# A streaming-encoder layer on one core: the last state-space unit is squeezed into twelve attention steps, the last fetch of its output moves from GpSimd's queue to SP's, and twenty low-part subtractions are queued behind a root

## The chip, the cores and the metric

The kernel runs on one core of one Trainium2 chip. The metric is the device time of one execution in microseconds. The time before is the median of three runs, 2292.37 us (2288.35 to 2292.53). The engines are called as in the profile: PE (TensorE), PEld (its weight loads), DVE (VectorE), ACT (ScalarE), POOL (GpSimd) and SP (SyncE, which issues most DMAs).

## What is computed

One layer over 2048 tokens of width 1024, in float32. Cut to what matters:

```python
h = rmsnorm(x, norm_mix_g);  proj = h @ w_in            # columns: u_ssm 512 | q 512 | k 512 | v 512
y_ssm = s5_mixer(u_ssm, ...)                            # 32 groups of 16 channels, one complex 64-state scan each
    # y = Re(C state) + D u;  y = gelu(y);  y = y * sigmoid(y @ w_glu + b_glu)
y_att = chunked_attention(q, k, v, rel_bias)            # 64-frame chunks, 8 chunks to the left, 8 heads
mixed = concat(rmsnorm(y_ssm, g1), rmsnorm(y_att, g2))
x  = x + mixed @ w_out
h2 = rmsnorm(x, norm_ffn_g)
x  = x + (silu(h2 @ w_gate) * (h2 @ w_up)) @ w_down
return rmsnorm(x, norm_final_g)
```

## The kernel before

**Precision and tiles.** Most products are made from float32 values split in two: a high part, cast by ACT (line 177, the helper `split`), and a low part, the raw value less the high one (line 178, on DVE or POOL). Each product is then three matmuls (line 77 is the helper through which PE's matmuls go, in program order; line 80 is the one for transposes). Tokens are worked on in four blocks `sb` of 512.

**Order.** All instructions of an engine run in one queue, in the order in which the program was laid out. PE's order, and that of the instructions issued through `k.V`, `k.A` and `k.Q`, is that of the code; the rest of DVE, ACT, POOL and SP is ordered by the scheduler of the framework, which has its own estimate of when an operand is ready. An instruction that waits holds back all that stands behind it on its engine.

**Attention with fillers.** `att_phase` runs 128 attention steps (block, pair of heads, head, 128 queries). A step's scores (`sc`) go from PE to DVE, which adds the bias `nb` and takes the minimum `mn` (line 858), then to ACT for the exponential (line 861). Two steps later PE transposes the result (`pt`), ACT copies its high part (`pth`, line 876), DVE its low part (`ptl`, line 877); after four steps `pv_head` multiplies by the values (`pj <- pth, ptl, v`; ACT `yt` line 900, DVE `ya` line 901). There is one buffer for `sc` and one for `pt`. Other work is put between the steps by `Unit.advance`: each unit is a generator with a first and a last step, and is carried on in proportion. Among the units are eight state-space units (`ssm_unit`, four groups each), one after the other, 15 steps each from step 2. One unit loads its tiles, makes `X` on PE and ACT, runs the scan on POOL (lines 617 to 629), sends the carried states to `XG` by four DMAs on POOL's queue (line 651), and after `YX` empty yields makes its output from eight matmuls, in turn `U, Tm` and `XG, Vm`. ACT copies that (line 661) and SP writes it to DRAM as `y` with eight DMAs (line 664).

**The mix phase.** At step `OPEN` = 119 `mix_phase` begins: SP loads the four row tiles of the GLU weights (`sg`, line 1006; two buffers), which ACT and DVE split into `wgh` and `wgl`. `load` fetches `y` in four tiles `f` of 128 channels (`yr`, line 1046), each by one DMA: for the first two blocks tiles 0 to 2 are on SP's queue and tile 3, which holds the channels of the last two units, is on POOL's. For the first two blocks the GELU is made of ACT square (line 1051), DVE (1052), ACT tanh (1053), DVE (1054), and its halves `gh` (ACT, line 1065) and `gl` (DVE, line 1066) are the operands of the GLU's matmuls (`pf <- gh, wgh` and so on), which PE runs between the last attention steps, tile 0 first.

**The third block's root and the gate.** After the output projection of a block (`w_out`, 2 x 24 matmuls for each of four column pairs `n`; DVE adds the residual in line 1140, SP stores it in line 1141, ACT squares it in lines 1143 to 1146, POOL adds up) `rstd_steps` makes the norm of that block: PE sums the squares (`big <- ones, sa`), `newton` makes the inverse root in ten small DVE instructions (lines 119 to 128, the last gives `no`), and PE spreads it by four transposes (`big <- ident, no`). For the third block (`sb` = 2) this lies inside the last block's output projection: the sum after `n` = 1 and the spread after `n` = 2. Behind `n` = 1 stands `build` as well, which fetches five of the seven first-half operands of the gate's product from DRAM (`lo <- hc`, line 1361, 5 x 4 DMAs) and splits them: twenty ACT casts (`hi`), twenty DVE subtractions (`lo`). The gate's first product then needs `hi`, `lo` and the split weights `c`; its first weight tile is cast by ACT and subtracted by DVE (line 178, `c <- raw`).

Of the kernel before, what the change touches and what calls it, by code (L numbers as in the profile page):

```python
# [16 lines left out]
P = 128  # L17
# [29 lines left out]
SL = 1  # L47
# [3 lines left out]
SW = 15  # L51
# [58 lines left out]
def f32(ap):  # L110
    return ap.bitcast(F32)
# [27 lines left out]
def spread(k, te, pb, o, c):  # L139

    for i in range(4):
        te.transpose(pb[:, i * P : (i + 1) * P], o[:, c + i : c + i + 1].to_broadcast([P, P]), k.ident[:])
# [525 lines left out]
SSM_N = YL + GP + 7 + 7 + 3 + 4  + YX + GP  # L668
# [24 lines left out]
def att_phase(k, ident, S):  # L693
    tc, nc, io = k.tc, k.nc, k.io
    with ExitStack() as cx:
# [245 lines left out]
        sp = tc.alloc_tile_pool(name="ssm", reuse_waits="tile", bufs=1)  # L941
        psum = cx.enter_context(tc.tile_pool(name="aps", bufs=1, space=bass.MemoryType.PSUM, reuse_waits="tile"))
        psum2 = cx.enter_context(tc.tile_pool(name="aps2", bufs=1, space=bass.MemoryType.PSUM, reuse_waits="tile"))
        units = []
# [9 lines left out]
                      Unit(qk_unit(sb, 2), QK_N, g0 + C[3], g0 + C[4], 2, light=LIGHT), Unit(v_unit(sb, 1), V_N, g0 + C[4], g0 + C[5], 2, light=LIGHT),  # L954
                      Unit(qk_unit(sb, 3), QK_N, g0 + C[5], g0 + C[6], 2, light=LIGHT)]
        for b in range(NG // GB):
            units.append(Unit(ssm_unit(k, sp, psum, S, b, k.ssm_eng), SSM_N, 2 + int(SW * b), 2 + int(SW * (b + 1)), light=SL))
        N = len(steps)
        for s in range(N + LAG + 2):
            if s == OPEN:  # L960
# [24 lines left out]
def mix_phase(k, S, bank):  # L985

    tc, nc, io = k.tc, k.nc, k.io
    te = k.te
    with ExitStack() as cx:
# [46 lines left out]
        yrs = [None]  # L1036

        def load(sb, early=False):
            b = B()
            b.o, b.early = {}, early  # L1040
            yt = k.t(my, "ys", [P, 4, SB], bufs=2)
            b.ys, b.g = [yt[:, f] for f in range(4)], []
            if sb % 2 == 0:
                yrs[0] = k.t(my, "yr", [P, 4, L, 128])
                for f in range(4):
                    (nc.gpsimd if sb == 0 and f == 3 else nc.sync).dma_start(yrs[0][:, f], S["y"][f * P : (f + 1) * P, :, sb * 64 : sb * 64 + 128])
            yv = yrs[0][:, :, :, (sb % 2) * 64 : (sb % 2 + 1) * 64]
            for f in range(4):
                if early:
                    t = k.t(mz, "tg", [P, L, SB // L], bufs=TGB)  # L1050
                    nc.scalar.activation(t[:], yv[:, f], AF.Square)
                    nc.vector.scalar_tensor_tensor(t[:], t[:], 1 / CUBE, yv[:, f], op0=ALU.add, op1=ALU.mult)
                    nc.scalar.activation(t[:], t[:], AF.Tanh, scale=CUBE * math.sqrt(2 / math.pi))
                    nc.vector.scalar_tensor_tensor(b.ys[f].rearrange("p (c j) -> p j c", j=L), t[:], 1.0, yv[:, f], op0=ALU.add, op1=ALU.mult)
                else:
                    nc.scalar.activation(yt[:, f].rearrange("p (c j) -> p c j", j=L), yv[:, f].rearrange("p j c -> p c j"), AF.Gelu_apprx_tanh)
            if sb != 1:
                halves(b)
            return b

        def halves(b):
            for f in range(4):
                gh, gl = k.t(my, f"gh{f}", [P, SB], F32R), k.t(my, f"gl{f}", [P, SB], F32R)
                if b.early:
                    nc.scalar.activation(gh[:], b.ys[f], AF.Copy, scale=0.5)
                    nc.vector.scalar_tensor_tensor(gl[:], b.ys[f], 0.5, f32(gh[:]), op0=ALU.mult, op1=ALU.subtract)
                else:
                    split(k, gh[:], gl[:], b.ys[f], nc.vector)
                b.g.append((gh, gl))
# [32 lines left out]
        def rstd2(b, c, pb):  # L1102

            for f, (y, g) in enumerate(zip((b.ya, b.ys)[c], (ga, gq if b.early else gs)[c : c + 1] * 4)):
                nc.vector.scalar_tensor_tensor(y, y, g[:, f : f + 1], pb, op0=ALU.mult, op1=ALU.mult)

        def big():
            return k.t(psum, *BIG)
# [10 lines left out]
        def mixed(b, c):  # L1119
            for n, (q, y) in enumerate(zip(QS[4 * c : 4 * c + 4], (b.ya, b.ys)[c])):  # L1120
                mt = k.t(mx, f"m{q}", [P, 2, SB], F32R)
                mh, ml = b.m[q] = mt[:, 0], mt[:, 1]
                split(k, mh, ml, y, nc.vector)
# [47 lines left out]
        b = load(0, True)  # L1171
# [26 lines left out]
        psum, mx = k.psum, k.mx  # L1198
# [6 lines left out]
        for sb in range(NSB):  # L1205
            if sb:
                b.m = {}
                mixed(b, 0)
            if sb == 0:
                held = [w_out(0, b, 2 * n) for n in range(2)]  # L1210
                next(held[0])
                ps = big()
                spread(k, te, ps[:, :512], b.o[1], 0)
                with tc.high_priority():
                    rstd2(b, 1, ps[:, :512])
                    mixed(b, 1)
                next(held[1])
            else:
                mixed(b, 1)
            for n in range(4):  # L1220
                if n == 0 and 0 < sb < NSB - 1:
                    nxt = next_block(sb + 1)
                if sb or n > 1:
                    for _ in w_out(sb, b, 2 * n):
                        pass
                else:
                    next(held[n])
                if n - (sb == NSB - 1) in (0, 1) and xr:
                    next(xr)
                if n in (1, 2) and sb + 1 < NSB:  # L1230
                    norm(nxt, n - 1)
                for _ in range(PRE0.get((sb, n), 0)):
                    next(pre)
                if (sb, n) == (NSB - 1, 1):
                    rx.close()
                    k.ga1 = tc.alloc_tile_pool(name="ga1", reuse_waits="tile", bufs=1, side="right")
                    k.gr = tc.alloc_tile_pool(name="gr", reuse_waits="tile", bufs=2, side="right")
                    wr = cx.enter_context(tc.tile_pool(name="wr2", reuse_waits="tile", bufs=2, side="right"))
                    k.hT = build(k, S, 0, k.ga1, EARLY)
            if sb < NSB - 1:  # L1240
                xr = rstd_steps(k, te, psum, k.mf, BIG, b.sa[:], D, S["rsn"][:, sb * SB : (sb + 1) * SB])
            if sb == 1:
                pre = pre_steps(k, S, 0, pre_tiles().__next__, True)
            k.last = b.sa[:]
            b = nxt
# [4 lines left out]
EARLY, LATE = (B11, T1, T2, B21, T3), (B22, T4)  # L1250
# [103 lines left out]
def build(k, S, hf, pool, ns):  # L1354

    hT = {}
    for n in ns:
        hi, lo = hT[n] = tuple(k.t(pool, f"{m}{n}", [P, 4, 512], F32R) for m in ("hi", "lo"))
        with k.tc.high_priority():
            for q in range(4) if hf == 0 else (slice(0, 4),):  # L1360
                k.nc.sync.dma_start(f32(lo[:, q]), S["hc"][hf, n, :, q])
        for q in range(4):
            split(k, hi[:, q], lo[:, q], f32(lo[:, q]), k.nc.vector)
    return hT
# [372 lines left out]
```

## Time and profile before

| What | Value |
|---|---|
| median of three runs | 2292.37 us (2288.35 to 2292.53) |
| the profiled execution: its time, its span | 2296.12 us, 2294.3 us |
| mean granted TensorE clock | 0.976 |
| busy: PE, PEld, DVE, ACT, POOL | 2180.3, 1835.1, 1490.5, 997.6, 1008.5 us |
| the chain that ended last: PE, DVE, issue, DMA | 76%, 8%, 6%, 5% |

The time is 1.8 us more than the span, which runs from the first to the last instruction. Times of single instructions below are microseconds from the span's start. In rows of the timeline, a bracket at the end holds the time for which the engine was idle before the row and what ended it; in rows of the waits stand the total, the number of times and the longest.

### The profile page before, as it was taken

The page shows a single profiled execution, that of the slowest core. Times are in us where ns is not written, and L with a number is a line of the kernel's source. Part 1 is how long each engine was busy: PE and PEld are TensorE (multiplying, and loading weights), DVE is VectorE, ACT ScalarE, POOL GpSimd, SP SyncE. Part 2 cuts the span into 40 slices and gives each one's busy share as a digit, 9 for nine tenths or more (in the row PEclk, how much of TensorE's full clock was granted, in tenths as well). Part 3 has the DMA queues.
Part 4 walks back from the last instruction along what each step waited for, and adds up shares of the span by engine and source line. Part 5 has one row for each costly group of instructions (what it writes and reads, how often), then busy time and mean ns, then how long its engine had stood idle before and what let it go on. Part 6 is the DMA issues. An engine that isn't in the chain of part 4 may idle for free.

```text
span 2294.3 us, 30408 instructions
## 1 busy us (share of the span) xinstructions
PE 2180.3 (95%) x10576; PEld 1835.1 (80%) x10576; DVE 1490.5 (65%) x2253; ACT 997.6 (43%) x1686; POOL 1008.5 (44%) x1215
## 2 busy tenths in 40 slices
PE   8978899899997999999999999999999999999998
PEld 6767688898986788778888887788888878888887
DVE  7845555656557755766775669766745376579576
ACT  6335455555556652343333335333333343345332
POOL 3406645356651121245555554555555414335450
PEclk9989999999998999999999999999999999999999
DMA  8887776676655334743554647454433297565552
GB/s 294 268 284 263 225 209 192 185 216 193 189 142 176 131 117 152 271 154 131 171 187 153 231 167 283 165 197 161 175 101 108 73 332 266 177 220 193 179 215 74
DMA packets 214769, 436.99 MB, mean 190 GB/s; under 512 B 27352, under 2 KB 57096, under 8 KB 207512
## 3 DMA queue, kind: packets, MB, share of 16 engines
q1 hardware_dynamic: 208728, 417.48, 54.8%
q0 software_dynamic: 5888, 17.58, 2.4%
q8 instruction: 83, 1.36, 0.3%
q14 instruction: 70, 0.57, 0.1%
HBM read 294.98 MB, written 132.15 MB: 186 GB/s over the span
## 4 chain that ended last, share of the span: by engine, by line
PE 76%; DVE 8%; issue 6%; DMA 5%; POOL 3%; ACT 2%; SPq 1%; DVEq 0%; POOLq 0%; ACTq 0%
PE X L77 19%; PE ps L77 18%; PE Y L77 10%; PE pf L77 8%; PE big L77 7%; PE W L77 5%; PE pj L77 4%; PE sc L77 2%; PE pt L80 2%; DMA xt<-in_xt 1%; DVE lo L178 1%; DMA lo<-hc 1%; DVE acc L1607 1%; SPq L579 1%; DMA w<-in_x 0%
## 5 line engine op out<-in xcount | busy, mean ns | idle before, releaser
L77 PE MATMUL X<-hi,c 128*128 128x512 f32 x1408 | 451.7, 391 | 5.0 <-ACT u L1415 2.9
L77 PE MATMUL ps<-hd,hd 128*128 128x512 f32 (+1 forms) x1968 | 428.2, 379 | 2.0 <-DVE hd L178 2.0
L77 PEld LDWEIGHTS ps<-hd,hd 128*128 128x128 f32 x1968 | 356.4, 188 | 72.4 <-DVE hd L178 3.1
L178 POOL TENSOR_TENSOR c<-S,c 128x512 fp32r<-128x512 f32 x172 | 246.4, 1435 | 268.9 <-ACT c L177 263.1
L77 PEld LDWEIGHTS X<-hi,c 128*128 128x128 f32 x1408 | 265.4, 189 | 62.6 <-ACT u L1415 4.9
L77 PE MATMUL X<-lo,c 128*128 128x512 f32 x704 | 274.9, 391 | 0.0
L178 POOL TENSOR_TENSOR hd<-hd 128x1536 fp32r<-128x1536 f32 (+1 forms) x46 | 157.0, 3416 | 215.3 <-ACT hd L177 204.4
L177 ACT CAST hd<-hd 128x1536 fp32r<-128x1536 f32 (+1 forms) x106 | 147.1, 1393 | 215.4 <-DMA hd<-hq 147.7
L178 POOL TENSOR_TENSOR c<-raw,c 128x512 fp32r<-128x512 f32 x129 | 185.8, 1441 | 123.5 <-ACT c L177 98.3
L77 PE MATMUL Y<-hi,c 128*128 128x512 f32 x704 | 225.7, 390 | 8.1 <-DVE u L1419 8.1
L1546 DVE TENSOR_TENSOR acc<-acc,ps 128x512 f32<-128x512 f32 x196 | 129.6, 682 | 77.8 <-PE ps L77 77.5
L77 PE MATMUL big<-m,woh 128*128 128x512 f32 x512 | 162.5, 399 | 1.4 <-DVE m L178 1.4
L77 PEld LDWEIGHTS Y<-hi,c 128*128 128x128 f32 x704 | 132.5, 188 | 37.7 <-DVE u L1419 10.2
L77 PE MATMUL pf<-hi,w 128*128 128x512 f32 x416 | 152.8, 420 | 7.4 <-ACT hi L741 3.9
L177 ACT CAST c<-S 128x512 fp32r<-128x512 f32 x176 | 109.4, 621 | 113.7 <-PE Y L77 51.3
L77 PEld LDWEIGHTS X<-lo,c 128*128 128x128 f32 x704 | 132.9, 189 | 27.4
L858 DVE CUSTOM_DVE_ANT_0 s<-sc,nb 128x640 f32<-128x640 f32 (+4 forms) x128 | 94.6, 739 | 91.5 <-PE sc L77 86.7
L617 POOL TENSOR_TENSOR st<-X,a 128x128 f32<-128x128 f32 (+2 forms) x136 | 46.0, 338 | 239.8 <-ACT X L603 204.7
L1415 ACT COPY u<-X 128x512 f32<-128x512 f32 x132 | 77.2, 584 | 159.8 <-PE X L77 159.8
L177 ACT CAST c<-raw 128x512 fp32r<-128x512 f32 x132 | 82.1, 622 | 139.9 <-PE Y L77 71.0
L178 DVE TENSOR_TENSOR hd<-hd 128x1536 fp32r<-128x1536 f32 (+1 forms) x60 | 118.1, 1969 | 30.6 <-ACT hd L177 30.2
L77 PE MATMUL Y<-lo,c 128*128 128x512 f32 x352 | 137.2, 390 | 0.0
(468 smaller groups left out, 4618.6 us busy)
## 6 DMA issues: line engine op xcount, KB each, us to landing
w<-wss SPq DMA_DIRECT2D x36, 1024.0 KB, 5.5
hq<-g SPq DMA_DIRECT2D x133, 256.0 KB, 2.1
hd<-hq SPq DMA_DIRECT2D x42, 768.0 KB, 4.5
hd<-wc SPq DMA_DIRECT2D x42, 768.0 KB, 6.0
raw<-in_w_gate SPq DMA_DIRECT2D x44, 512.0 KB, 3.8
raw<-in_w_up SPq DMA_DIRECT2D x44, 512.0 KB, 4.1
wc<-px SPq DMA_DIRECT2D x66, 256.0 KB, 3.2
wss<-w SPq DMA_DIRECT2D x12, 1024.0 KB, 5.6
```

The lines of the kernel that those rows point to most:

```text
L77: return self.tc.keep_in_program_order(self.tc.nc.tensor.matmul(*a, **b))
L80: return self.tc.keep_in_program_order(self.tc.nc.tensor.transpose(*a, **b))
L177: (hi_eng or nc.scalar).copy(hi, raw)
L178: (lo_eng or nc.gpsimd).tensor_tensor(lo, raw, f32(hi), op=ALU.subtract)
L579: ins = nc.sync.dma_start(out, in_)
L617: eng.tensor_tensor(t[:, :, :, :n], src, ar, op=ALU.mult)
L858: nc.vector.tensor_tensor_reduce(s[:, :nk].rearrange("p (a b) -> p a b", a=nch), ps[:, :nch, :half], hd.nb[:, nk - 1 :: -1].rearrange("p ( ...
L1415: nc.scalar.copy(u[:], ps[:])
L1546: V.tensor_tensor(a, a, ps[:], op=ALU.add)
L1607: nc.vector.scalar_tensor_tensor(v, v, k.go[:, i : i + 1], rs, op0=ALU.mult, op1=ALU.mult)
```

## The change

Three edits. First, the last step of a state-space unit is capped at 119; only the last unit (steps 107 to 122) is shortened by it, to twelve steps. Second, all four tiles of `y` go through SP's queue. Third, `build` for the first half runs inside `tc.issue_after(k.root)`, which puts every instruction of the block that runs on the root's engine, DVE, behind the root: `k.root` is at that place the last instruction of the third block's `newton`. The block's DMAs and ACT casts are not on DVE and are not held.

```diff
-            units.append(Unit(ssm_unit(k, sp, psum, S, b, k.ssm_eng), SSM_N, 2 + int(SW * b), 2 + int(SW * (b + 1)), light=SL))
+            units.append(Unit(ssm_unit(k, sp, psum, S, b, k.ssm_eng), SSM_N, 2 + int(SW * b), min(2 + int(SW * (b + 1)), 119), light=SL))
...
-                    (nc.gpsimd if sb == 0 and f == 3 else nc.sync).dma_start(yrs[0][:, f], S["y"][f * P : (f + 1) * P, :, sb * 64 : sb * 64 + 128])
+                    nc.sync.dma_start(yrs[0][:, f], S["y"][f * P : (f + 1) * P, :, sb * 64 : sb * 64 + 128])
...
-                    k.hT = build(k, S, 0, k.ga1, EARLY)
+                    with tc.issue_after(k.root):
+                        k.hT = build(k, S, 0, k.ga1, EARLY)
```

What it moves is seen in the order of the queues. On PE only the last unit's eight output matmuls move. In the kernel before, this stands on PE before them (the end of the last unit of key projections is above the first row; `sc` are scores, `pt` transposes):

```order
L77 MATMUL sc_8173<-k_1720_7352,q2l_7351 128x320
L80 MATMUL pt_8182<-ident_81,s_8077 128x128 x5
L77 MATMUL sc_8230<-k_1845_7976,q2h_7974 128x320
L77 MATMUL sc_8230<-k_1845_7976,q2l_7975 128x320
...
L80 MATMUL pt_8240<-ident_81,s_8124 128x128 x5
...
L80 MATMUL pt_8257<-ident_81,s_8178 128x128 x5
L77 MATMUL pj_8266<-U_7536,Tm_7547 128x256
L77 MATMUL pj_8266<-XG_2371,Vm_7556 128x256
...
L77 MATMUL sc_8289<-k_1845_7976,q2h_7974 128x320
```

In the changed kernel the same place on PE reads (`pf <- hi, w` are the last key projections):

```order
L77 MATMUL pf_8084<-lo_1554_6550,w_7883 128x512
L77 MATMUL pf_8084<-hi_1553_6549,w_7883 128x512
L77 MATMUL pj_8173<-U_7536,Tm_7547 128x256
L77 MATMUL pj_8173<-XG_2371,Vm_7556 128x256
...
L77 MATMUL pj_8179<-U_7536,Tm_7547 128x256
L77 MATMUL pj_8179<-XG_2371,Vm_7556 128x256
L77 MATMUL sc_8194<-k_1720_7352,q2h_7350 128x320
...
L80 MATMUL pt_8203<-ident_81,s_8093 128x128 x5
L77 MATMUL sc_8251<-k_1857_8012,q2h_8010 128x320
```

The eight matmuls have moved up past three score groups and three groups of transposes (27 instructions), directly behind the last key projection. On POOL nothing of the unit moves: its scan and its four `XG` DMAs stand where they did, and only the fetch of `y` is gone from its queue.

ACT's and DVE's orders change from there to the first GLU output. On ACT the kernel before has, around the transposes of the last head but one (`tg` the GELU, `gh` GLU operands; tiles 0 to 2 done, tile 3 at the end):

```order
L1065 ACTIVATE gh_1937_8368<-ys_8338 128x512
L1065 ACTIVATE gh_1939_8372<-ys_8338 128x512
L876 CAST pth_8322<-pt_8440 128x5x128
L861 ACTIVATE s_8429,sm_8237<-s_8429,mn_8430 128x640
L876 CAST pth_8322<-pt_8457 128x5x128
L861 ACTIVATE s_8453,sm_8237<-s_8453,mn_8454 128x640
L876 CAST pth_8322<-pt_8481 128x5x128
L861 ACTIVATE s_8477,sm_8237<-s_8477,mn_8478 128x640
L1026 ACTIVATE sq_8409<-ya_1948_8401 128x512
L1029 ACTIVATE sg_8411<-ya_1949_8402 128x512
L1051 ACTIVATE tg_8359<-yr_8339 128x512
```

The changed kernel has on ACT, at the same transposes:

```order
L876 CAST pth_8322<-pt_8440 128x5x128
L177 CAST wgh_1903_8239<-sg_8241 128x512
L876 CAST pth_8322<-pt_8457 128x5x128
L177 CAST wgh_1906_8245<-sg_8247 128x512
L1051 ACTIVATE tg_8349<-yr_8339 128x512
L861 ACTIVATE s_8453,sm_8258<-s_8453,mn_8454 128x640
L1053 ACTIVATE tg_8349<-tg_8349 128x512
L1051 ACTIVATE tg_8354<-yr_8339 128x512
L1065 ACTIVATE gh_1937_8368<-ys_8338 128x512
L1051 ACTIVATE tg_8359<-yr_8339 128x512
L1053 ACTIVATE tg_8354<-tg_8354 128x512
```

The GELU of tiles 1 and 2 has moved behind the transposes `pt_8457`, together with that of tile 3 and of the next block, and the exponentials and copies of the steps 8477 and 8481 stand behind all of these; DVE's order follows the same pattern. On SP the eight writes of `y` now stand ahead of the last two GLU weight loads, of the bias load `nb` for the next head and of the fetches of tiles 1 to 3.

On DVE, at the third block's root, the kernel before has the low parts in between (`lo_2249` and so on are the five operands, four subtractions each; line 1140 is the output projection's eviction):

```order
L1140 TENSOR_TENSOR xt_10152<-xt_10152,big_10154 128x1024
L178 TENSOR_TENSOR lo_2249_10339<-lo_2249_10339,hi_2248_10338 128x512
...
L178 TENSOR_TENSOR lo_2257_10395<-lo_2257_10395,hi_2256_10394 128x512
L178 TENSOR_TENSOR lo_2255_10381<-lo_2255_10381,hi_2254_10380 128x512
L119 TENSOR_SCALAR nv_10307<-big_10302 128x4
L1140 TENSOR_TENSOR xt_10246<-xt_10246,big_10248 128x1024
L120 TENSOR_SCALAR ny_10309<-nv_10307 128x4
...
L128 SCALAR_TENSOR_TENSOR no_10310<-nf_10308,ny_10309 128x4
...
L1140 TENSOR_TENSOR xt_10408<-xt_10408,big_10410 128x1024
L178 TENSOR_TENSOR lo_2249_10339<-lo_2249_10339,hi_2248_10338 128x512
L1140 TENSOR_TENSOR xt_10470<-xt_10470,big_10472 128x1024
```

The changed kernel has on DVE:

```order
L1140 TENSOR_TENSOR xt_10152<-xt_10152,big_10154 128x1024
L1140 TENSOR_TENSOR xt_10246<-xt_10246,big_10248 128x1024
L119 TENSOR_SCALAR nv_10307<-big_10302 128x4
...
L128 SCALAR_TENSOR_TENSOR no_10310<-nf_10308,ny_10309 128x4
L178 TENSOR_TENSOR lo_2249_10339<-lo_2249_10339,hi_2248_10338 128x512 x2
...
L178 TENSOR_TENSOR lo_2249_10339<-lo_2249_10339,hi_2248_10338 128x512
L178 TENSOR_TENSOR lo_2255_10381<-lo_2255_10381,hi_2254_10380 128x512
L178 TENSOR_TENSOR lo_2257_10395<-lo_2257_10395,hi_2256_10394 128x512 x4
L1140 TENSOR_TENSOR xt_10408<-xt_10408,big_10410 128x1024
L1140 TENSOR_TENSOR xt_10470<-xt_10470,big_10472 128x1024
```

The root and the eviction of `xt_10246` now stand ahead of all twenty low parts, and the eviction of `xt_10408` behind all twenty; before, 19 of them were ahead of it. The last cast on ACT is that of `lo_2249`; five subtractions now stand behind the one that waits for it, where before it was the last one. ACT's and SP's orders are the same there.

## The prediction

> **What bounds the kernel now.** I read first the busy times on the page, then the waits of PE over the span and over the stretch 640 to 800 us, and then the timelines of the engines at the two places that the change touches.
>
> ```profile
> PE 2180.3 (95%) x10576; PEld 1835.1 (80%) x10576; DVE 1490.5 (65%) x2253; ACT 997.6 (43%) x1686; POOL 1008.5 (44%) x1215
> ```
>
> PE is busy for 95% of the span. So a change counts where it takes a wait of PE away or makes one; work that the other engines do earlier or later is free as long as PE is not kept waiting by it. The waits of PE over the span that touch the change are these:
>
> ```profile
> PE pf L77 <- ACT gh L1065: 6.2, 1, 6.2
> PE big L80 <- DVE no L128: 4.8, 1, 4.8
> PE pf L77 <- DVE gl L1066: 2.6, 1, 2.6
> PE X L77 <- DVE c L178: 2.1, 1, 2.1
> ```
>
> The first and third are for tile 3 of the GELU, which the first two edits mean to bring earlier. The second is for the root of the third block, which the third edit brings earlier. The fourth lies behind it, where the gate's first product begins. Between the last unit of key projections and the first GLU product there are also these, in the waits of the stretch 640 to 800:
>
> ```profile
> PE sc L77 <- DVE mn L858: 4.5, 3, 2.2
> PE pt L80 <- DVE ptl L877: 2.4, 1, 2.4
> ```
>
> They are the attention steps themselves: `sc` and `pt` have one buffer each, so PE waits until DVE has taken the last one out. The timeline of PE there:
>
> ```profile
> 692.69 0.31 PE L77 MATMUL sc<-k,q2h 128*128 128x320 f32 x1
> ...
> 699.94 1.06 PE L77 MATMUL pj<-U,Tm 128*128 128x256 f32 x2
> ...
> 703.84 0.50 PE L77 MATMUL sc<-k,q2h 128*128 128x320 f32 x1
> ...
> 711.28 1.22 PE L80 MATMUL pt<-ident,s 128*128 128x128 f32 x5 [2.41 <-DVE ptl L877]
> 714.75 0.63 PE L77 MATMUL sc<-k,q2h 128*128 128x320 f32 x1 [2.25 <-DVE mn L858]
> 717.06 0.78 PE L77 MATMUL pf<-gh,wgh 128*128 128x512 f32 x1
> ...
> 733.97 0.63 PE L77 MATMUL pj<-pth,v 128*128 128x512 f32 x1
> ```
>
> At 692.69 the key projections are over. The last unit's eight output matmuls run from 699.94 to 703.84, the first GLU product begins at 717.06, and the last head's values product (`pv_head`) at 733.97. I use this last one as the mark at which early or late is measured. The waits of PE in the stretch 744 to 940 behind it are these:
>
> ```profile
> PE big L77 <- DVE wol L178: 1.6, 2, 0.8
> PE big L77 <- DVE m L178: 1.4, 1, 1.4
> PE big L77 <- DVE nv L119: 1.1, 3, 0.6
> ```
>
> They are 4.1 us in all, each for DVE, which would run late along with PE; so I carry a delay at the mark through unchanged.
>
> **Edit 1: the cap at step 119.** It moves the eight matmuls 27 instructions up, to 692.69, and brings nothing of the unit forward on POOL. What they read comes from here (POOL's timeline, and the landing of the two DMAs in the view of the tile `XG`):
>
> ```profile
> 693.59 1.21 POOL L651 DMA_DIRECT2D XG<-X  x2 [0.30 <-POOL X L629]
> ```
>
> ```profile
> DMA to landing us min/median/max: 4.3/4.4/4.5
> ```
>
> The last of the two is issued at about 694.2 and lands 4.5 us later, at 698.7. Before, that was hidden: `U, Tm` began at 699.94. Now the first two pairs can run on the states that were sent earlier, from 692.69, and then PE stands still from about 694.0 to 698.75, **4.8 us**, with 27 instructions queued behind that need none of it. So the unit is moved ahead of its data. The eight matmuls take 3.9 us in the rows above; the half that is left, and the half clock that a stall of this length leaves behind (below, at 974.89, it is seen), put the next scores at about 702.3.
>
> From 692.69 to 717.06 PE has spent 24.4 us, 3.9 of it on the eight matmuls: 20.5 us for the six pairs of scores and transposes, one values product and the rest. Of these, 6.9 us were waits (2.2 on the first two `mn`, 2.41 and 2.25 in the rows above). All of them could go at best (13.6 us), or none (20.5). I take off 2.2 us: the long wait for `ptl` at 711.28, since the GELU work that stood ahead of it on DVE has moved away; each `mn` and each `ptl` is still waited for. That is 18.3 us, and puts the first GLU product at 702.3 + 18.3 = 720.6, against 717.06.
>
> From there DVE decides. In its new order the GELU of tiles 1 to 3 and of the next block stands behind the transposes of step 8457, and the `ptl` of step 8481, which the last values product needs, behind all that. The durations come from DVE's timeline before:
>
> ```profile
> 694.22 0.82 DVE L858 CUSTOM_DVE_ANT_0 s<-sc,nb 128x640 f32<-128x640 f32 x1
> ...
> 694.97 0.82 DVE L877 TENSOR_TENSOR ptl<-pt,pth 128x640 fp32r<-128x640 f32 x1
> ...
> 705.97 1.30 DVE L178 TENSOR_TENSOR wgl<-sg,wgh 128x512 fp32r<-128x512 f32 x2
> ...
> 712.07 1.88 DVE L1066 SCALAR_TENSOR_TENSOR gl<-ys,gh 128x512 fp32r<-128x512 f32 x3
> ...
> 723.61 1.89 DVE L1052 SCALAR_TENSOR_TENSOR tg<-tg,yr 128x512 f32<-128x512 f32 x3
> 725.41 2.95 DVE L1054 SCALAR_TENSOR_TENSOR ys<-tg,yr 128x512 f32<-128x512 f32 x3
> ```
>
> Start to start that is 0.75 for `s` and for `ptl`, 0.6 for `wgl`, L1052 and L1066, and 1.0 for L1054. From the `ptl` of 8457 to that of 8481 DVE has two `ptl` (1.5), one `wgl` (0.6), two `s` (1.5), seven L1052 (4.2), seven L1054 (7.0), three L1066 (1.8) and two sums of squares of the same size (1.2): 17.8 us, and I add 1.1 for the places where it waits for ACT's halves. It begins some 1.1 us behind the first GLU product, at 721.7, so the mark comes at 721.7 + 18.9 = 740.6, against 733.97: **+6.6 us**. The waits for `gh` and `gl` (8.8 us) are not saved by this; the same DVE work stands in front of the mark, only later and in one piece, and PE waits there instead. With the two ends of the stretch before (13.6 and 20.5) it is +1.9 and +8.8. I take the value near the upper end because the single buffers of `sc` and `pt` are the same.
>
> **Edit 2: tile 3 through SP.** Before, it was fetched late on POOL:
>
> ```profile
> 710.67 0.93 POOL L1046 DMA_DIRECT2D yr<-y  x1 [15.87 <-DVE ya L901]
> ```
>
> Now all fetches but tile 0's stand on SP behind the eight writes of `y`, the last two weight loads and `nb`. By the walk above they are issued at about 709, and their first reader stands behind the transposes at 720. What hides them is the attention steps; I cost it at 0. If the first values came so early that this cover went, tile 3's reader would wait for its fetch, by 4.5 us at most if it lands as slowly as `XG` does.
>
> **Edit 3: the low parts behind the root.** The rows at the third root, by engine:
>
> ```profile
> 974.89 1.09 PE L80 MATMUL big<-ident,no 128*128 128x128 f32 x4 [4.75 <-DVE no L128]
> ...
> 990.28 0.73 PE L77 MATMUL X<-hi,c 128*128 128x512 f32 x2 [2.07 <-DVE c L178]
> ```
>
> ```profile
> 958.14 0.95 PE L77 MATMUL big<-ones,sa 128*128 128x1 f32 x8
> ```
>
> ```profile
> 968.59 0.16 DVE L119 TENSOR_SCALAR nv<-big 128x4 f32<-128x4 f32 x1
> ...
> 974.65 3.70 DVE L178 TENSOR_TENSOR lo<-lo,hi 128x512 fp32r<-128x512 f32 x6
> 978.26 1.22 DVE L1140 TENSOR_TENSOR xt<-xt,big 128x1024 f32<-128x1024 f32 x1
> 979.40 1.59 DVE L178 TENSOR_TENSOR lo<-lo,hi 128x512 fp32r<-128x512 f32 x1
> ...
> 989.54 0.69 DVE L178 TENSOR_TENSOR c<-raw,c 128x512 fp32r<-128x512 f32 x1
> ```
>
> The sum of squares is ready at 959.1, the root starts at 968.59 and is interleaved with low parts until 974.7. In the new order it stands ahead of all of them: ten instructions of 0.16 us, at most 0.3 each with the hand-over, end at about 961.6, eight microseconds before PE asks for it. The wait of 4.75 us goes, and with it the half clock behind it:
>
> ```profile
> 975.00:980.00 5.00, 5.00 (x19) 4.17 (x20) 5.00 (x8) 3.34 (x5) 0.86 (x1) 0.73 0.42 161
> ```
>
> The granted clock is 0.73 in these five microseconds (the column behind the five engines), which is 1.35 us lost. Together **6.1 us** by which PE reaches the gate's first product earlier. The Trainium skill, "TensorE: Matmul & The Clock Gate", section "What's actually happening", has the clock halved after an idle window of about 3.4 us and for about as long; by it the loss would be 1.7 us, an estimate from that page, where the row gives 1.35.
>
> What is late next is the path to the first weight tile, and the edit lengthens it:
>
> ```profile
> 967.33 9.59 ACT L177 CAST hi<-lo 128x512 fp32r<-128x512 f32 x15 [1.22 <-DMA lo<-hc]
> ...
> 982.27 1.06 ACT L1146 ACTIVATE xt<-xt 128x1024 f32<-128x1024 f32 x1 [3.55 <-DMA x<-xt]
> 983.23 0.60 ACT L177 CAST c<-raw 128x512 fp32r<-128x512 f32 x1
> ```
>
> ```profile
> 979.14 1.30 POOL L1147 TENSOR_TENSOR sa<-sa,xt 128x512 f32<-128x512 f32 x1 [14.44 <-issue]
> ```
>
> ```profile
> 979.51 0.37 SPq L1141 DMA_DIRECT2D x<-xt  x1
> ```
>
> The eviction of `xt_10408`, at 978.26 before, is now queued behind all twenty low parts. Five of them follow the last cast, which ends at 976.92; at 0.6 each that is 980.0, so the eviction is 1.75 us later. Its store (979.51), the square that waits for the store (982.27) and the cast of `c` queued behind that square on ACT (983.23, ending 983.83) all shift with it. Then the low part of `c` (0.69) and PE's third `X` matmul: 983.83 + 1.75 + 0.69 is 986.3 at the best, 4.0 us earlier than 990.28. At the worst two low parts are held up as the one at 979.40 was (1.59 for 0.69, beside POOL's 979.14), and the low part of `c` stands behind two POOL additions of 1.3 that follow the same square: 990.4, a gain of nothing (+0.1). I take one hold-up of 0.9 at each place: 988.1, **−2.2 us**. So two thirds of the 6.1 us turn into a wait of PE for the first weight tile.
>
> The Trainium skill, "SBUF — State Buffer", section "Who interferes with whom", says that a DVE instruction with two SBUF inputs and a GpSimd instruction that reads SBUF exclude each other, and that whichever was issued first blocks the other for its whole length. This speaks against the change, since it puts the low parts and POOL's additions side by side; the row at 979.40 agrees. With each of them blocked by a whole POOL instruction the sum for this edit would be about nothing, the worst case above.
>
> **The sum.** +6.6 + 0 − 2.2 = +4.4 us. The profiled execution took 2296.12 us, 3.75 above the median of the runs, and would become 2300.5; the median of 2292.37 becomes **2296.8**. A measurement of this kernel can tell about 0.2%, or 4.6 us, from no change, so the forecast lies just inside that bound; this case alone, with the ends of its two terms not both met at once, reaches from +1 to +8 us (2293.4 to 2300.4).
>
> **The rivals.** *Faster: the lateness is made good before the GLU.* PE's own work between the scores after the unit and the first GLU product is about 9.5 us (20.5 less 6.9 of waits and about 4 of half clock). If DVE and ACT, freed of the early GELU, kept up with that, the GLU would begin at 711.8 and the mark would come at 731.8, −2.2 us; with a good outcome of the third edit, −2.9, that is −5.1: 2287.3. For it speaks that some 5 us of DVE work leave this stretch; against it the one buffer each of `sc` and `pt`, which forces PE to wait in nearly every pair. It decides if PE's waits between the unit and the first GLU product sum to under about 1 us. Chance 0.18.
>
> *No change: the third edit pays in full.* If the eviction starts before about 978.3, because the low parts keep closer to the casts, nothing is late behind the root and 6.1 us come in: +0.5, 2292.9. Against it: five subtractions stand behind the last cast in the order. Chance 0.17.
>
> *Slower than forecast: the states land later and the low parts are blocked.* The fetch of tile 0 and the weight loads now go out on SP while `XG` is on its way; each microsecond of delay of `XG` is one of PE's. With 1.3 us of that and a gain of nothing from the third edit it is +7.9: 2300.3. It decides if `XG` lands after 700. For it: that landing already takes 4.3 to 4.5 us here. Chance 0.15.
>
> **How the numbers follow.** The forecast case keeps 0.50, half of it beyond +4.6 us. Faster by over 0.2% is the first rival, 0.18; within 0.2% are the second and half of the forecast case, 0.17 + 0.25 = 0.42; slower are the other half and the third rival, 0.40. The range goes from 2287.0, which holds about half of the first rival, to 2301.0, which holds about half of the third: some 0.16 is left out.
>
> **What would show it.** Right: a wait of PE on the DMA of `XG` of 4 to 5 us, scores after it at about 702; the first GLU product near 720.6 and the values product near 740.6, DVE without a gap between; the wait for `no` gone, the clock full behind it, and a new wait of PE of some 4 us at the gate's first product, with `xt_10408` evicted at 980 or later. Wrong: no wait for `XG`, which would mean that POOL's scan or its DMAs ended earlier; the values product before 734; no wait at the gate's first product.

## The result and the profile after

| | before | changed |
|---|---|---|
| median of 22 runs | 2289.95 us (2284.8 to 2296.02) | 2296.73 us (2289.25 to 2304.54) |
| ratio | | 1.0031, 95% interval 1.0023 to 1.0039 |
| profiled execution, span | 2294.3 us | 2300.1 us |

The change makes the kernel slower by 0.31%, which by this ratio is 7.1 us (5.3 to 8.9). The forecast was +4.4 us for the likeliest case, with a range of that case from +1 to +8. The waits of PE over the span in the changed kernel:

```profile
PE pf L77 <- ACT gh L1065: 5.0, 1, 5.0
PE pj L77 <- issue: 4.8, 1, 4.8
...
PE X L77 <- ACT c L177: 3.2, 1, 3.2
...
PE pf L77 <- DVE gl L1066: 0.6, 1, 0.6
...
PE X L77 <- DVE c L178: 0.2, 1, 0.2
```

The row for `no` (4.8 us before) is gone, and a wait of 3.2 us for the cast of the first weight tile has come. The waits for `gh` and `gl` have shrunk from 8.8 to 5.6 us together. A wait of 4.8 us at `pj`, which the profile can put down to no engine ("issue"), is new. The timeline of PE shows where it lies:

```profile
687.76 0.39 PE L77 MATMUL pf<-hi,w 128*128 128x512 f32 x1
687.99 0.59 PE L77 MATMUL pj<-U,Tm 128*128 128x256 f32 x2
693.34 0.79 PE L77 MATMUL pj<-XG,Vm 128*128 128x256 f32 x2 [4.76 <-issue]
...
695.23 1.19 PE L77 MATMUL pj<-XG,Vm 128*128 128x256 f32 x2 [0.25 <-DMA XG<-X]
...
698.23 0.50 PE L77 MATMUL sc<-k,q2h 128*128 128x320 f32 x1
...
715.67 0.78 PE L77 MATMUL pf<-gh,wgh 128*128 128x512 f32 x1
...
734.49 0.63 PE L77 MATMUL pj<-pth,v 128*128 128x512 f32 x1
736.23 0.80 PE L77 MATMUL pj<-ptl,v 128*128 128x512 f32 x1 [1.11 <-DVE ptl L877]
...
740.56 1.20 PE L80 MATMUL pt<-ident,s 128*128 128x128 f32 x5
```

The last unit's output begins right behind the last key projection (687.76), does its first `U, Tm` (a row `x2` here is one matmul of the program, which the trace holds as two instructions), and stands still until the states are there. The view of the tile `XG` gives the landing of the four DMAs, the last of which POOL issued at 689.57 and which took the 5.5 us:

```profile
DMA to landing us min/median/max: 2.3/3.3/5.5
```

The same places of the kernel before, in its timeline of PE:

```profile
692.46 0.39 PE L77 MATMUL pf<-hi,w 128*128 128x512 f32 x1
...
734.39 0.63 PE L77 MATMUL pj<-ptl,v 128*128 128x512 f32 x1
...
737.10 0.73 PE L80 MATMUL pt<-ident,s 128*128 128x128 f32 x5
```

PE's queue is the same in both kernels up to the last key projection, and the changed one reaches it 4.7 us sooner (687.76 against 692.46): two executions drift apart by that much, so times are compared within a stage. From the last key projection to the transposes behind the last values product, called stage A below, it is 737.10 − 692.46 = 44.6 us before and 740.56 − 687.76 = 52.8 us after: 8.2 us more.

At the third root the changed kernel has on DVE, ACT, POOL and PE:

```profile
962.27 1.22 DVE L1140 TENSOR_TENSOR xt<-xt,big 128x1024 f32<-128x1024 f32 x1 [5.88 <-PE big L77]
...
966.15 0.69 DVE L178 TENSOR_TENSOR lo<-lo,hi 128x512 fp32r<-128x512 f32 x1
969.91 1.89 DVE L178 TENSOR_TENSOR lo<-lo,hi 128x512 fp32r<-128x512 f32 x3 [3.07 <-ACT hi L177]
972.50 9.84 DVE L178 TENSOR_TENSOR lo<-lo,hi 128x512 fp32r<-128x512 f32 x16 [0.69 <-ACT hi L177]
982.26 1.21 DVE L1140 TENSOR_TENSOR xt<-xt,big 128x1024 f32<-128x1024 f32 x1
...
988.40 1.41 DVE L178 TENSOR_TENSOR c<-raw,c 128x512 fp32r<-128x512 f32 x1 [1.28 <-ACT c L177]
```

```profile
965.41 12.25 ACT L177 CAST hi<-lo 128x512 fp32r<-128x512 f32 x19 [0.22 <-DMA lo<-hc]
...
986.80 1.06 ACT L1146 ACTIVATE xt<-xt 128x1024 f32<-128x1024 f32 x1 [7.32 <-DMA x<-xt]
```

```profile
979.62 3.89 POOL L1147 TENSOR_TENSOR sa<-sa,xt 128x512 f32<-128x512 f32 x1 [13.60 <-issue]
```

```profile
961.92 0.95 PE L77 MATMUL big<-ones,sa 128*128 128x1 f32 x8
...
973.75 0.60 PE L80 MATMUL big<-ident,no 128*128 128x128 f32 x4
...
988.42 0.80 PE L77 MATMUL X<-hi,c 128*128 128x512 f32 x1 [3.16 <-ACT c L177]
```

The spread of the root (973.75) waits for nothing. But DVE waits 3.1 and 0.7 us for two certain casts, has done four low parts when ACT has done twelve casts, and works off the other sixteen in one piece until 982.3. Behind them come the eviction, the store, the square at 986.80, which waited 7.3 us for that store, and the weight cast for which PE waits. In this pair of profiles the stretch from the sum of squares to the gate's third `X` matmul is 990.28 − 958.14 = 32.1 us before and 989.87 − 961.92 = 28.0 after, a seeming gain of 4.2 us. The experiments show that this difference isn't the edit's.

### The profile page after: what moved, and what is told of

Same layout as the page of the kernel before. It is cut to its first block, busy times and chain, and to the rows that moved or that the text cites. A ratio compares the mean times of both kernels' runs of the same rounds, so it can differ in the third digit from the quotient of the medians.

```text
span 2300.1 us, 30392 instructions
## 1 busy us (share of the span) xinstructions
PE 2189.1 (95%) x10576; PEld 1839.0 (80%) x10576; DVE 1486.1 (65%) x2253; ACT 1000.3 (43%) x1686; POOL 1003.4 (44%) x1214
## 4 chain that ended last, share of the span: by engine, by line
PE 76%; DVE 8%; issue 5%; DMA 4%; POOL 4%; ACT 2%; SPq 2%; DVEq 0%; POOLq 0%; ACTq 0%
PE ps L77 20%; PE X L77 20%; PE Y L77 10%; PE pf L77 7%; PE big L77 7%; PE W L77 5%; PE pj L77 4%; PE pt L80 2%; PE sc L77 2%; DVE lo L178 1%; DMA lo<-hc 1%; DMA xt<-in_xt 1%; SPq L579 1%; POOL X L620 1%; POOL X L619 1%
```

## The experiments

Each kernel is timed against the kernel before on the same chip; the ratio is to it. Two stages are read from the profile of each: stage A as above, and stage C from the sum of squares of the third block (`big <- ones, sa`) to the gate's first `Y` matmul.

**The three edits alone.** `e1_cap` has the cap only, `e2_root` the root only, `e3_sp` the fetch through SP only.

```diff
# e1_cap
-    2 + int(SW * b), 2 + int(SW * (b + 1)), light=SL
+    2 + int(SW * b), min(2 + int(SW * (b + 1)), 119), light=SL
# e2_root
-    k.hT = build(k, S, 0, k.ga1, EARLY)
+    with tc.issue_after(k.root):
+        k.hT = build(k, S, 0, k.ga1, EARLY)
# e3_sp
-    (nc.gpsimd if sb == 0 and f == 3 else nc.sync).dma_start(yrs[0][:, f], ...
+    nc.sync.dma_start(yrs[0][:, f], ...
```

> Only the cap at step 119. Theory: the cap is the whole loss; aligned instruction by instruction, the two profiles differ by 9.2 us more behind the GLU than ahead of the last unit's output matmuls, so this kernel is slower than before by 7 to 10 us (ratio about 1.0037), with the 4.8 us wait for XG and the half clock at the last values product. Rival: part of the loss belongs to the third edit, since the profiles also drift apart by 6 us behind the gate's first product; then the cap alone costs only about 4 us (1.0018).

> Only the low parts behind the root. Theory: it gains the 2 to 4 us read at the gate's first product, ratio about 0.9987; the wait for the root is gone and a wait of some 3 us for the first weight tile stands in its place. Rival: the gate's later steps run late because of it, and it is 1 to 3 us slower than before (1.0004 to 1.0013).

> Only the fetch of tile 3 through SP. Both theories: no change, within 1 us (ratio 0.9996 to 1.0004): the fetch comes behind the eight writes of y on the same queue at about 708 instead of 710.7 on POOL, and its reader stands at 722.

Measured: 1.0012 (0.9997 to 1.0027), 0.9992 (0.9981 to 1.0003) and 0.9983 (0.9970 to 0.9997). The root tells nothing from no change. The fetch through SP is a small gain where none was expected. The cap came out lower than expected, and the three together at −0.13%, where the whole has +0.31%. So I took two of the edits to work against each other, and ran the pairs.

**The pairs.** They combine the lines above: `e12_cap_root`, `e13_cap_sp`, `e23_sp_root`; the second was run twice (`e13b_cap_sp`), and the cap alone a second time (`e1b_cap`).

> Cap and root without the fetch through SP. The three single edits came to +0.12%, -0.08% and -0.17%, together -0.13%, where the whole change has +0.31%: two of them work against each other. Theory: cap and root. Alone, the cap's 7 us are partly given back at the wait for the third root (in its profile that wait is 1.5 us instead of 4.8), because the low parts are paced by their fetches and not by PE; with the root moved ahead there is nothing left to give back. Then this kernel is as slow as the whole change, ratio 1.002 to 1.0035. Rival: cap and SP work against each other (the fetch of tile 3 behind the writes of y); then this one is at 0.9995 to 1.0010.

> Cap and fetch through SP without the root. Theory (cap and root work against each other): like the cap alone or a little better, ratio 0.9995 to 1.0015, with a wait for the third root of 1 to 2.5 us. Rival (cap and SP do): as slow as the whole change, 1.002 to 1.0035, with the values product of the last head 1 us or more later than in the cap alone.

> Fetch through SP and root without the cap: the change without the edit that is held to be its loss. Theory: 2 to 6 us faster than before, ratio 0.9975 to 0.9990, and the key projections followed by scores with no wait for XG. Rival (root and SP gain nothing, the single runs were noise): 0.9995 to 1.0005.

> Cap and SP once more, on the same chip as the kernel with the earlier scan, which it is to be compared with, and as the cap alone. Both theories: 1.002 to 1.0035 as before.

> The cap alone once more, since its interval before (0.9997 to 1.0027) does not tell whether it loses less alone than with SP or root. Theory of one loss (the cap costs the same 6 to 8 us with and without the other edits, the first run was low by chance): ratio 1.002 to 1.0035. Rival (the other edits each make the cap worse): 1.0005 to 1.0015 again, 3 us or more below cap and SP.

Measured: cap and root 1.0033 (1.0020 to 1.0047); cap and SP 1.0035 (1.0020 to 1.0050) and 1.0024 (1.0012 to 1.0035); SP and root 0.9992 (0.9974 to 1.0011); the cap again 1.0030 (1.0015 to 1.0044). SP and root lie between their two expectations, and the interval holds both. My theory of cap and root working against each other falls: without the root, cap and SP are as slow. That two edits work against each other at all falls with the second run of the cap, at 1.0030. Every kernel with the cap is slow by about the same, 1.0024 to 1.0035 but for that first run, whose interval reaches to 1.0027; every kernel without it isn't. The cap is the loss. The table has the stages of all of them ("fetch" is how long before the sum of squares SP begins to fetch the operands, `lo <- hc`; "waits" are PE's for `no` and for the first weight tile):

| kernel | stage A | stage C | fetch | waits |
|---|---|---|---|---|
| before | 44.6 | 35.7 | 2.1 | 4.8 + 2.1 |
| `e3_sp` | 41.6 | 36.1 | 2.1 | 5.0 + 2.1 |
| `e2_root` | 42.8 | 31.5 | 4.6 | 0 + 3.7 |
| `e23_sp_root` | 42.1 | 35.8 | 2.4 | 0 + 6.8 |
| `e1_cap` | 52.1 | 30.8 | 4.5 | 1.5 + 2.1 |
| `e1b_cap` | 52.5 | 29.6 | 4.6 | 1.2 + 2.1 |
| `e13_cap_sp` | 52.7 | 28.8 | 5.6 | 0.3 + 2.1 |
| `e13b_cap_sp` | 52.1 | 36.2 | 1.9 | 4.9 + 2.1 |
| `e12_cap_root` | 52.9 | 34.3 | 1.8 | 0 + 6.2 |
| changed | 52.8 | 32.3 | 4.2 | 0 + 3.4 |

Stage A is 41.6 to 44.6 us without the cap (39.9 and 45.9 in two more kernels without it, below) and 52.1 to 52.9 with it, whatever else is changed. Stage C goes by the column "fetch" and not by the edit. The two executions of cap and SP, one program on two chips, show it. Their sums of squares, and their waits of PE in this stretch, the first execution ahead:

```profile
957.54 0.95 PE L77 MATMUL big<-ones,sa 128*128 128x1 f32 x8
```

```profile
PE big L80 <- DVE no L128: 0.3, 1, 0.3
```

```profile
961.35 0.95 PE L77 MATMUL big<-ones,sa 128*128 128x1 f32 x8
```

```profile
PE big L80 <- DVE no L128: 4.9, 1, 4.9
```

and the fetches on SP in the two, in the same order:

```profile
951.90 14.82 SPq L1361 DMA_DIRECT2D lo<-hc  x20
```

```profile
959.46 14.88 SPq L1361 DMA_DIRECT2D lo<-hc  x20
```

Where the fetch starts 5.6 us ahead of the sum, the root is late by 0.3 us; where it starts 1.9 ahead, by 4.9. So the wait for `no` that the edit takes away is the lateness of the fetches: the low parts, and the root between them, are done when their operands have come. With the root ahead of them, PE passes the root and waits the same time for the first weight tile, whose cast is behind the same low parts: with a late fetch 6.8, 7.0 and 7.0 us of waits without the root edit, 6.8 and 6.2 with it; with an early one 3.6, 3.3 and 2.4 without, 3.7 and 3.4 with it.

A late fetch goes along with a slow addition on POOL. The fetch stands on SP behind loads of `xt` (line 1132), which wait for POOL's two additions of an earlier column pair: 3.1 us at the longest in the first execution, 6.7 in the second. The first of the two additions, in the same order:

```profile
931.41 1.31 POOL L1147 TENSOR_TENSOR sa<-sa,xt 128x512 f32<-128x512 f32 x1 [11.75 <-issue]
```

```profile
934.71 4.93 POOL L1147 TENSOR_TENSOR sa<-sa,xt 128x512 f32<-128x512 f32 x1 [12.82 <-issue]
```

In the first execution it is all but over when DVE begins four subtractions (`m`, line 178) at 932.55; in the second these begin at 934.78, beside it. It took 4.9 us in all five executions of the table in which the fetch starts about 2 us ahead of the sum, and 1.3 us in the other five. How the delay gets from the loads to the fetch, some 17 us later on SP, isn't followed further here.

**The eviction ahead of the last low parts.** `e6_rootev` is the root edit with one more line, `e236` that and the fetch through SP. On DVE the eviction of `xt_10408` then stands ahead of the last six low parts.

```diff
-            nc.vector.tensor_tensor(xt[:], xt[:], ps[:], op=ALU.add)
+            with tc.high_priority() if (sb, i) == (NSB - 1, 4) else ExitStack():
+                nc.vector.tensor_tensor(xt[:], xt[:], ps[:], op=ALU.add)
```

> The third edit alone, with one more: the eviction of xt_10408 is scheduled with priority, which puts it ahead of the last six low parts on DVE instead of behind all twenty. Theory (the eviction behind the low parts is what eats two thirds of the 6.1 us): the eviction starts near 977 instead of 982, the wait for the first weight tile falls from 3.2 us to about nothing, and the kernel gains 2 to 4 us over the third edit alone (ratio about 0.9974 to before). Rival (the low parts themselves are what the first product waits for): no difference to the third edit alone.

> Fetch through SP, root, and the eviction of xt_10408 ahead of the last six low parts, without the cap: the version that should beat both. Theory: the SP fetch is worth 2 to 3 us ahead of the GLU, the root with the eviction 4 to 6 us; ratio 0.996 to 0.9985. Rival: what is won at the root is waited for later in the gate, since the weights there come at their own pace; 0.9990 to 1.0005.

Measured: 1.0004 (0.9988 to 1.0020) and 0.9981 (0.9967 to 0.9995). The first is no gain over the root alone. The wait for the weight tile's cast is gone, and PE's waits in this stretch are now, in `e6_rootev`:

```profile
PE X L77 <- DVE c L178: 3.6, 1, 3.6
```

It is the low part of the same tile: DVE has the six remaining low parts ahead of it (in `e236` the same wait is 5.1 us). So the rival holds: the low parts themselves are what the first product waits for. `e236` beats the kernel before by 4 us, but no more than the fetch through SP alone (0.9983).

**The same end with the data ahead.** `e7_early` has the cap and SP, and lets the last unit begin three steps sooner. Its output stands on PE exactly where the cap puts it, with the orders of ACT and DVE of cap and SP around it; only the products that feed its scan stand earlier.

```diff
-    2 + int(SW * b), 2 + int(SW * (b + 1)), light=SL
+    2 + int(SW * b) - (3 if b == 7 else 0), min(2 + int(SW * (b + 1)), 119), light=SL
```

> Cap and fetch through SP, and the last unit begins three steps earlier (104 to 119, fifteen steps again), without the root. On PE the unit's output stands exactly where the cap puts it, and ACT and DVE have the same order; only the products that feed the scan stand earlier, so the states arrive before they are asked for. Theory (the wait for XG, 4.8 us, and the half clock behind it are most of the cap's loss): no wait for XG, and the stretch from the last key projection to the end of the last values product is 5 to 7 us shorter than in cap and SP together (52.7 us there), ratio to before 0.9995 to 1.0015. Rival (the order of the GELU behind the wait is the loss; the wait only uses up time that would be waited later): that stretch shrinks by less than 2 us and the ratio stays at 1.0025 or more.

Measured: 1.0074 (1.0060 to 1.0089), and stage A 46.0 us. The last key projection and what follows it on PE:

```profile
702.63 0.39 PE L77 MATMUL pf<-hi,w 128*128 128x512 f32 x1
702.86 0.59 PE L77 MATMUL pj<-U,Tm 128*128 128x256 f32 x2
703.29 0.59 PE L77 MATMUL pj<-XG,Vm 128*128 128x256 f32 x2
...
706.13 0.50 PE L77 MATMUL sc<-k,q2h 128*128 128x320 f32 x1
...
723.76 0.48 PE L77 MATMUL pf<-gh,wgh 128*128 128x512 f32 x1
...
744.29 0.80 PE L77 MATMUL pj<-ptl,v 128*128 128x512 f32 x1 [1.12 <-DVE ptl L877]
...
748.61 1.23 PE L80 MATMUL pt<-ident,s 128*128 128x128 f32 x5
```

No wait stands between `U` and `XG`, and stage A is 6.1 to 6.7 us shorter than in the two executions of cap and SP. That is the 5 to 7 us of the theory. All of it lies ahead of the first GLU product, which comes 21.1 us behind the last key projection, against 27.8 and 27.4 us with cap and SP and 23.2 to 24.6 us without the cap. Behind it nothing is won: from there to the values matmul that needs the last `ptl` it is 20.5 us here, 20.6 in cap and SP (both executions) and in the changed kernel, and 14.4 to 18.3 us in the kernels without the cap. The values product takes 4.3 us here too. So the cap has two costs in this stage: the wait for `XG`, and the new order of ACT and DVE, which is the rival's part and costs the same with and without that wait. The ratio was missed altogether, for a reason outside the stage: the earlier start makes two long waits, where unit 7 now meets unit 6 (the timeline of PE, 630 to 660 us):

```profile
639.08 1.19 PE L77 MATMUL pj<-U,Bst 128*128 128x256 f32 x2 [5.66 <-DMA Tm<-kts]
...
653.57 1.12 PE L80 MATMUL pj<-ident,rb 128*128 128x128 f32 x4 [9.67 <-ACT X L603]
```

They are 15.3 us. Over 20 to 680 us the two kinds of wait come to 19.3 us, where the kernel before has 5.2; that is about what the total is over the expected one.

**All units a little shorter.** `e5_sw146` has no cap, but 14.6 steps for each unit (`SW = 14.6`), with SP and root as in the change.

> Instead of the cap every state-space unit gets 14.6 steps instead of 15, so that the last one also ends by step 119 but begins three steps earlier, its scan with it; fetch through SP and root as in the change. Theory (the cap loses because the last unit's output is moved ahead of its data, and the end at 119 as such is harmless): no wait for XG at the last unit, the GELU of tile 3 ahead of the GLU, the values product of the last head earlier than in the change by 5 us or more; ratio to before 0.997 to 0.999. Rival (the early end itself loses, by the order of ACT and DVE that comes with it): 1.001 to 1.003, with the wait for gh and mn as long as in the change.

Measured: 1.0065 (1.0042 to 1.0089); stage A 43.8 us. There is no wait for `XG` at the last unit, so the stage doesn't have the cap's loss, but it isn't better than without the cap either (41.6 and 42.1 with SP), and the total missed both expectations. The waits of PE from 20 to 700 us tell why:

```profile
PE pj L77 <- DMA XG<-X: 9.4, 4, 5.3
...
PE pj L77 <- DMA U<-u: 7.8, 3, 3.5
```

In the changed kernel the same two are 3.0 and 2.8 us: the units before the last now ask for their states and inputs too early. It reaches the last key projection at 700.8 us, where the kernels in the table reach it between 683 and 692.

## Why the prediction was right and where it was wrong

**Direction and size.** The forecast was +4.4 us, half of its case beyond 0.2%; measured is +7.1 us, 0.31%. Its term of +6.6 for the cap is 8.2 in stage A, and of its term of −2.2 for the root the runs show nothing. With these two the sum would be +8.2, inside the interval of 5.3 to 8.9. That the forecast time, 2296.8 us, is met by the measured median to 0.1 us is luck: the median of the kernel before is 2289.95 over 22 runs, 2.4 us below that of the three runs from which the forecast was added up.

**The cap: right, and somewhat too small.** The unit was moved ahead of its data, as the step said. The stall was forecast at 4.8 us and is 4.76 + 0.25, but its course was read wrongly, and that the size fits is in part luck. The step let PE work for 1.3 us on states that had been sent earlier. By line 651 each of the four transfers carries one half of the states for two of the unit's four groups, and POOL sends the second halves last; so each group needs one of the last two transfers, and PE stands still after the first `U, Tm`, 0.6 us on. It goes on at 693.34, when the third transfer lands (issued at 688.94, 4.3 us to landing), and at 695.23, when the fourth does (5.5 us, where 4.5 were taken). From the last key projection the first GLU product comes 3.3 us later than before (715.67 − 687.76 against 717.06 − 692.46), forecast 3.5. The values matmul that needs the last `ptl` comes 6.5 us later (736.23 − 687.76 against 734.39 − 692.46), forecast 6.6; by the prediction's own mark, the first matmul of the values product, it is 5.2 us (734.49 − 687.76 against 733.97 − 692.46). What the step left out is behind that mark: it took the values product to need the same time as before, but it runs from 736.23 to 740.56, 4.3 us, where the same matmuls took 2.7 (734.39 to 737.10). The granted clock (the column behind the five engines) was 0.50 there, behind a stretch of 0.59; the stretch before the change and the product itself had 0.70 and 0.78. In the changed kernel:

```profile
715.60:734.40 18.80, 10.15 (x30) 7.06 (x30) 16.48 (x24) 15.37 (x29) 1.27 (x1) 0.59 0.32 122
734.40:740.60 6.20, 5.09 (x19) 4.24 (x18) 3.12 (x6) 1.89 (x4) 0.00 (x0) 0.50 0.68 202
```

and before:

```profile
717.00:734.00 17.00, 8.27 (x31) 6.46 (x31) 13.54 (x20) 11.80 (x22) 1.68 (x1) 0.70 0.51 185
734.00:737.00 3.00, 3.00 (x17) 2.73 (x16) 1.04 (x3) 1.55 (x3) 0.00 (x0) 0.78 0.54 156
```

The step that said that DVE decides from the first GLU product to the mark is well supported. It gave 20.0 us for that stretch, and 20.6 were measured; DVE was busy for 16.5 of the 18.8 us in the first row above; and `e7_early` takes 20.5 us although its first GLU product comes over 6 us sooner. Its values product takes 4.3 us as well, so neither hangs on the stall. That ACT, busy for 15.4 of the 18.8 us, has no part in it isn't shown.

**The fetch through SP: right in the change, wrong by itself.** With the cap it costs and gains nothing (stage A 52.1, 52.5 and 52.9 without it, 52.7, 52.1 and 52.8 with it). Without the cap the stage is shorter with it (41.6, 42.1 and, in `e236`, 39.9 against 44.6, 42.8 and, in `e6_rootev`, 45.9), in single executions that differ by up to 3 us among themselves; the ratios are 0.9983, 0.9992 and 0.9981, and the second can't be told from no change. The prediction costed it only behind the cap. The gain isn't an earlier fetch: without the cap SP fetches tile 3 22 to 23 us behind the last key projection, where POOL fetched it after 17 to 18. But PE's waits for `gh` and `gl` are 5.0 and 0.9 us in the three kernels with it, 6.2 and 1.5 to 2.6 us in the three without; why, no run here shows.

**The root: the mechanism was right, its price was not.** The wait for `no` went, the eviction of `xt_10408` came behind all low parts, and a wait for the first weight tile took its place, as forecast. The step that failed is that PE gains 6.1 us of which 3.9 are eaten. Alone the edit can't be told from no gain (0.9992, interval 0.9981 to 1.0003), though by itself this interval doesn't exclude the −2.2 us either. Against it speak the other kernels: with the root added, SP goes from 0.9983 to 0.9992, the cap from 1.0012 and 1.0030 to 1.0033, cap and SP from 1.0035 and 1.0024 to 1.0031; and with the fetch at the same place the waits of PE are about the same with and without it. No gain is the worst end of the bounds that the prediction gave. It counted five subtractions behind the last cast, as if DVE had done all the others by then. But in its new order DVE waits for two casts and then has sixteen left; the eviction starts 982.26 − 977.66 = 4.6 us after the last cast (which ended at 965.41 + 12.25), where 3.1 were forecast. The other hold-ups came in part: the low part of `c` took 1.41 us beside POOL's addition, about the one hold-up that was taken, but it was POOL that was held up by the low parts, 3.89 us for an addition of 1.30, and not they by it. The Trainium skill's rule that was weighed there ("SBUF — State Buffer", section "Who interferes with whom") agrees with the first row, and with the second in that the two exclude each other; but it has one instruction block the other for that instruction's length, and here the addition was held up for 2.6 us by subtractions of 0.61 us; the measurement decides. More than that, the 4.75 us themselves are no fixed sum: they go from 0.3 to 5.0 us between executions without the root edit, with the time at which the operands' fetches start.

**The rivals.** That the lateness would be made good before the GLU didn't happen: PE's waits between the unit and the first GLU product sum to 5.0 us, where this rival asked for under 1. That the third edit pays in full didn't happen either. The slower rival, +7.9, came nearest to the measured +7.1, and with much of its mechanism: the third edit shows no gain, and the last transfer of `XG` landed about 1 us later than expected (1.3 in the rival). What the rival doesn't have is the slow values product.

**What stays open.** What puts POOL's addition beside DVE's subtractions in some executions, where the fetches start some 2 us ahead of the sum of squares, and ahead of the subtractions in others, where they start 4 to 6 us ahead; both are seen with and without each of the edits. The first run of the cap alone (1.0012) differs from the second (1.0030) by less than their intervals, and is put down to chance, not explained.

## What to carry to other kernels

To bring a result forward, move its slowest input first: an output that is moved up in PE's order ahead of its data makes everything behind it wait. The work on the other engines that reads it changes its place as well; here that cost PE some microseconds more, with or without the wait. A wait on the profile is a gain only if what it waits for isn't paced by something that the next consumer waits for as well; here the root and the first weight tile both hung on the same fetched operands. A difference of a few microseconds in a stage between two profiles should be looked for between two executions of one program before it is put down to an edit.

## What was not expected of the hardware

Sixteen subtractions back to back on DVE (9.84 us) stretched one POOL addition from 1.30 to 3.89 us without being slowed themselves (0.61 us each). The same happens some 27 us ahead of the third block's sum of squares, where an addition takes 4.9 us instead of 1.3 in five of the table's ten executions, and the fetch of the operands on SP starts 2 to 4 us later in these. And the granted clock stayed at half for the whole values product of 4.3 us, on 0.50 in the row above, though PE was busy for 5.1 of those 6.2 us; the same product ran at 0.78 before.
